# Second layer of a hybrid DiT step: three heads and a convolution projected ahead of the norm, and a norm in two VectorE instructions a tile

## The chip, the cores and the metric

One Trainium2 chip, one core. The metric is the device time of one launch in microseconds (us), the median of the runs of a kernel. Tiles are written partitions x elements.

## The reference

One inference step of a diffusion backbone: two layers, model width 1024, 384 tokens (128 context, 256 latent) that use the same weights but are modulated by two different vectors (two groups). Each layer norms its input and reads it through one input projection with three kinds of heads, adds their output projection, and then an MLP of width 4096 with a squared ReLU. All is float32.

```
h = _rmsnorm(x, norm_mix[d]) * (1.0 + c_scale) + c_shift
q, k, v, gb, gc, xin, u, vs = _project(h, w_in[d])
# latent tokens: rotary on q, k; cached context keys and values in front
att  = _diff_attention(q, k, v, lam, subln[d], lam_init)   # 4 heads, softmax of two halves, a0 - lam * a1
conv = gb * _short_conv(gc * xin, conv_w[d], conv_b[d])    # 256 channels, width 3
cmlp = _chunk_mlp(u, vs, w_s[d], b_s[d])
x = x + gate * (concat([att, conv, cmlp]) @ w_out[d])
h = _rmsnorm(x, norm_mlp[d]) * (1.0 + c_scale2) + c_shift2
x = x + gate2 * (relu(h @ w_up[d]) ** 2 @ w_down[d])
```

The outputs are the two normed token groups and the new context keys and values.

## The kernel before

Activations lie transposed, as 8 tiles of 128 features x 384 tokens. Float32 products are made of three float32r matmuls: an operand is split into a high part (a rounding cast) and a low part (operand minus high part), and `mm3` adds high·high, low·high and high·low. The split activation is held in `hh` (high) and `hl` (low). Weights are streamed in chunks of 512 KB, one for each 128 output columns of a projection: a DMA on SP's queue into one of six `raw` buffers, a ScalarE cast to `whi` (L201) and a VectorE subtraction to `wlo` (L203), four buffers each.

Each engine runs its instructions in the order in which the program writes them, and that order is made by hand. The TensorE stream is written straight down; after each product of three matmuls `tick` advances a clock, and work of the other engines, written as generators, is started with a delay in ticks (`start(gen, delay)`) and goes on when its `yield n` ticks have passed. The delays stand in the table `WAIT`, one number a layer. A projection of a 128-column tile (`proj_tiles`) has 8 ticks, one for each k tile of 128 features. The V projection (`proj_tokens(a, 512)`, tile `nat`) has tokens as rows: for each of 8 k tiles 9 matmuls of 512 columns, counted as 4 ticks, 72 matmuls and 32 ticks in all. It is evicted by three ScalarE copies into `v_t` (L887).

The norm. While the layer ahead ends, `scaled_high` and `scaled_low` put x·scale, split but not yet divided by the root mean square, into `hh` and `hl`, with two more columns for the shifts of the two groups (386 = `TE` columns). A projection of these, times rstd (a row over tokens), plus the projected shift, equals the projection of the normed input. So the key and query tiles `pkq` of the first `NPRE` heads are projected from the un-normed `hh`, `hl`, and `evict` multiplies by rstd. `normed` later replaces `hh`, `hl` by the normed input, tile by tile: on VectorE t = x·scale·rstd (two instructions, one a token group, L362), on ScalarE hh = t + shift (two, L370), on VectorE hl = t + shift − hh (two, L373). Whatever is projected behind that reads the normed input. In the second layer before the change, two heads (four `pkq` tiles) go ahead; `first_heads` adds their projected shifts on ScalarE (L706 to L712) and starts `keys` and `queries`: the rotary part (a VectorE shuffle and three GpSimd instructions), and the splits `kh`, `kl`, `qs` in halves of 64 partitions. Then follow V, the two later heads (`pk`, `pq`), and two convolutions (`pgc`, `pxi`, `pgb` for each).

Attention (`attention`) of a head is three units: 128 context queries, and twice 128 latent queries over 384 keys. A unit has scores `sc` in two PSUM buffers (two halves of the differential softmax), a VectorE maximum `nm`, ScalarE exps `e` with sums `s`, a ScalarE scaling of the second half, a VectorE combination of `e`, three TensorE transposes `pt`, and a ScalarE copy of them (`atp`, `ats`). The third unit goes on with `po`, the product with `v_t`, its norm and transpose. `sc` and `pt` share three PSUM buffers: unit 1's second score tile takes the first buffer of unit 0, and unit 2's two score tiles those of unit 1. The units of head h start at `unit0` + h·`head` ticks, 8 ticks apart.

The MLP's `hidden` evicts a tile of the up projection: VectorE copies the two shift columns to `ub` and multiplies by rstd, ScalarE applies ReLU with the shift as bias (two instructions), squares and casts.

Of the kernel before, what the change touches and what calls it, by code (L numbers as in the profile page):

```python
# [15 lines left out]
P = 128  # L16
# [3 lines left out]
TP = 128  # L20
# [8 lines left out]
NPRE = (3, 2)  # L29
# [33 lines left out]
    "fh0": (14, 14),  # L63
# [8 lines left out]
    "normed": (3, 3),  # L72
    "wait_normed": (1, 12),
    "mix": (4, 4),
    "heads": (4, 1),
# [5 lines left out]
    "head": (24, 24),  # L81
    "late": (0, 5),
# [18 lines left out]
def dit_kernel(ctx, tc, xT, cT, wmod, wmodT, wall, ck, cv, ws, lam, bs_in, small, rope, ident_in, yT, kT_out, v_out):  # L101
# [112 lines left out]
    def temp(name):  # L214
        return work.tile([P, T], F32, name=name, tag="tA", bufs=4)
# [129 lines left out]
    def rstd_of_x():  # L345
        pm = misc_tile("pstat")
        mm(pm[:, 0:T], ones_d, stat["acc"], start=True, stop=True)
        y = stat["rstd"] = work.tile([P, T], F32, name="rstd", bufs=1)
        yield 2
        nc.scalar.activation(y, pm[:, 0:T], AF.Ln)  # L350
        nc.scalar.activation(y, y, AF.Exp, scale=-0.5)
        yield 2
        a = work.tile([P, T], F32, name="rtmp", tag="rtmp", bufs=1)
        rsqrt_refined(y, a, pm[:, 0:T])

    def normed(scale, shift, every):


        def times(dt):
            t = temp("t")  # L360
            for g, a, b in GROUPS:
                nc.vector.scalar_tensor_tensor(  # L362
                    t[:, a:b], x[:, dt, a:b], scale[:, dt, g : g + 1], stat["rstd"][:, a:b], ALU.mult, ALU.mult
                )
            return t

        t = times(0)
        for dt in range(KT):
            for g, a, b in GROUPS:
                nc.scalar.activation(hh[:, dt, a:b], t[:, a:b], AF.Identity, bias=shift[:, dt, g : g + 1])  # L370
            ahead = times(dt + 1) if dt + 1 < KT else None
            for g, a, b in GROUPS:
                nc.vector.scalar_tensor_tensor(  # L373
                    hl[:, dt, a:b], t[:, a:b], shift[:, dt, g : g + 1], hh[:, dt, a:b].bitcast(F32),
                    ALU.add, ALU.subtract,
                )
# [132 lines left out]
    for d in range(DEPTH):  # L509
# [26 lines left out]

        if d == 0:
# [68 lines left out]
            start(shifted(), 1)  # L608
            start(steps(spread, 4, 3), wt["spread"])
            start(rstd_of_x(), wt["rstd"])  # L610
            q_t, k_t, v_t, cv_t, wsT, vsn = mixer_tiles()
# [12 lines left out]
        else:  # L624
# [20 lines left out]
        def split_y(i, yf):  # L645
            nc.scalar.copy(y[:, 0, i], yf)
            yield wt["sy"]
            nc.vector.tensor_sub(y[:, 1, i], yf, y[:, 0, i].bitcast(F32))

        LO, HI = slice(0, 64), slice(64, 128)  # L650
        parts = {}

        def rope_apply(t):
            rt = work.tile([P, 2, TS], F32, name="rt", tag="rope", bufs=1)
            s, t1 = rt[:, 0], rt[:, 1]
            nc.vector.stream_shuffle(s, t, [(i + 16) % 32 for i in range(32)])
            nc.gpsimd.tensor_mul(t1, t, rp[:, 0])
            nc.gpsimd.tensor_mul(s, s, rp[:, 1])  # L658
            nc.gpsimd.tensor_add(t, t1, s)

        def keys(h):


            k = k_t[:, h % 3]
            nc.sync.dma_start(k[:, TP : 2 * TP], ck[d, h])
            nc.sync.dma_start(kT_out[d, h], k[:, 0:TP])
            yield wt["k0"]
            rope_apply(k[:, 2 * TP :])
            yield wt["k1"]
            kh = work.tile([P, 2, T], F32R, name="kh")  # L670
            kl = kl_t[h % 2]
            parts[h] = [kh, kl]
            for c, own in enumerate((LO, HI)):
                nc.scalar.copy(kh[own, c], k[own, TP:])
            yield wt["k2"]
            for c, (own, other) in enumerate(((LO, HI), (HI, LO))):
                nc.scalar.copy(kh[other, c], k[own, TP:])
                nc.vector.tensor_sub(kl[own, c], k[own, TP:], kh[own, c].bitcast(F32))

        def queries(h):  # L680


            q = q_t[:, h % 3]
            yield wt["q0"]
            rope_apply(q[:, TP:T])
            yield wt["q1"]
            qs = work.tile([P, 2, TS], F32R, name="qs")
            parts[h].append(qs)
            for c, own in enumerate((LO, HI)):
                nc.scalar.copy(qs[own, c], q[own, TP:T])  # L690
            yield wt["q2"]
            for c, (own, other) in enumerate(((LO, HI), (HI, LO))):
                nc.vector.tensor_sub(qs[other, c], q[own, TP:T], qs[own, c].bitcast(F32))

        def first_heads():
            for h in range(NPRE[d]):
                if h != 1:
                    if d == 0:
                        yield from shift_products(raws, bias, 2 * h, 2 * h + 4 - h)
                    qb = bias[:, 2 * h + 1 : 2 * h + 4 - h : 2]  # L700
                    nc.vector.tensor_scalar_mul(qb, qb, 0.125)
                if h == 2:
                    yield wt["fh0"]
                for g, s0, s1, off in KSEG:
                    kk = k_t[:, h, off : off + s1 - s0]
                    nc.scalar.activation(kk, kk, AF.Identity, bias=bias[:, 2 * h, g : g + 1])  # L706
                go(keys(h))
                yield wt["fh1"]
                qb = bias[:, 2 * h + 1]
                for c, own in enumerate((LO, HI)):  # L710
                    nc.scalar.activation(qp_t[h % 3][own, c], q_t[own, h, 0:TP], AF.Identity, bias=qb[own, 0:1])
                nc.scalar.activation(q_t[:, h, TP:T], q_t[:, h, TP:T], AF.Identity, bias=qb[:, 1:2])  # L712
                yield wt["fh2"]
                go(queries(h))
                yield wt["fh3"]
# [118 lines left out]
        def conv(ct):  # L834

            pg = proj_tiles(a, name="pgc")
            gc = work.tile([P, T], F32, name="gc", tag="tB", bufs=2)
            nc.scalar.copy(gc, pg[:, 0:T])
            px = proj_tiles(a, name="pxi")
            cz = work.tile([P, T + 1], F32, name="cz", tag="tB", bufs=2)  # L840
            go(conv_input(ct, gc, px, cz))
            pb = proj_tiles(a, name="pgb")
            go(conv_output(ct, pb, cz))
# [26 lines left out]
        start(first_heads(), wt["heads"])  # L870
        if d == 0:
            nc.sync.dma_start(bs, bs_in)
# [39 lines left out]
        for f in range(2):  # L912
# [199 lines left out]
```

## Time and profile before

| | us |
|---|---|
| median of 3 runs | 909.0 (907.77 to 909.69) |
| profiled execution | 906.61 |
| its span, first to last instruction | 904.8 |
| mean granted TensorE clock | 0.995 |

| engine | busy us | share of the span |
|---|---|---|
| TensorE, matmuls | 876.9 | 97% |
| TensorE, weight loads (beside them) | 841.8 | 93% |
| VectorE | 651.6 | 72% |
| ScalarE | 481.7 | 53% |
| GpSimd | 84.2 | 9% |

In the profile's lines PE is TensorE, DVE VectorE, ACT ScalarE, POOL GpSimd, and SP the queue that issues DMAs. A row of groups has source line, engine, operation, tile written <- tiles read, shapes and count, then busy us and mean ns of one, then idle time of the engine just before them and what ended it. A row of waits has the engine, the tile at which it stood, what it waited for, then us in total, times and the longest. A row of the timeline has start us, length us, engine, line, operation and count. A row of windows has the stretch, its length, busy us (and instructions) of the engines, the granted clock as a share of full speed, the DMA share and GB/s. Matmul records overlap, so what one costs is the distance of starts. Source lines in rows of before are those of the kernel above.

The second layer's mixer runs from about 460 us on; its V projection and the norm beneath it lie around 480 to 510 us, the later heads and convolutions to about 570. The MLPs, about 200 to 450 and from 600 on, are the bulk of the time.

### The profile page before, as it was taken

How to read it: one execution, taken by the hardware profiler on the slowest of the kernel's cores; microseconds unless marked ns; L12 is line 12 of the kernel's file. 1: busy time of each engine (PE TensorE's matmuls, PEld its weight loads, DVE VectorE, ACT ScalarE, POOL GpSimd, SP SyncE). 2: the span in 40 equal slices, each digit the busy share in tenths (PEclk: the TensorE clock that was granted, in tenths of full speed). 3: DMA queues.
4: the chain of work that ended last, by engine and by line, in shares of the span. 5: the costliest groups of instructions: out<-in, count | busy, mean ns of one | idle time of the engine just before them, and what ended most of it. 6: DMA issues, size and time to landing. Idle time of an engine off the chain costs nothing.

```text
span 904.8 us, 14504 instructions
## 1 busy us (share of the span) xinstructions
PE 876.9 (97%) x5476; PEld 841.8 (93%) x5476; DVE 651.6 (72%) x1214; ACT 481.7 (53%) x949; POOL 84.2 (9%) x84
## 2 busy tenths in 40 slices
PE   5999989999999999999998999999999999999996
PEld 4867878999999999999997889999999999999996
DVE  5697887889888777889979877568886334555333
ACT  4568765447662236654336786444675223665331
POOL 1013310030000000000113340002000000000021
PEclk9999999999999999999999999999999999999998
DMA  9977657555667655557663323234565333433302
GB/s 346 330 280 258 231 168 271 167 166 167 205 190 235 230 187 190 197 189 236 213 218 102 131 73 117 92 97 134 175 220 167 123 133 117 133 124 118 116 1 70
DMA packets 48470, 156.55 MB, mean 173 GB/s; under 512 B 5392, under 2 KB 11024, under 8 KB 48400
## 3 DMA queue, kind: packets, MB, share of 16 engines
q1 hardware_dynamic: 48400, 155.63, 51.8%
q8 instruction: 43, 0.70, 0.3%
q14 instruction: 27, 0.22, 0.1%
HBM read 152.98 MB, written 2.62 MB: 172 GB/s over the span
## 4 chain that ended last, share of the span: by engine, by line
PE 84%; DVE 7%; ACT 4%; POOL 2%; issue 1%; DMA 1%; SPq 0%; DVEq 0%; ACTq 0%; POOLq 0%
PE pdn L220 10%; PE pdn L222 10%; PE pdn L221 10%; PE pup L221 10%; PE pup L220 9%; PE pup L222 9%; PE po L220 2%; PE po L221 2%; PE po L222 2%; PE pm L262 2%; PE pkq L220 2%; PE pkq L221 2%; PE pkq L222 1%; DVE wlo L203 1%; POOL rt L658 1%
## 5 line engine op out<-in xcount | busy, mean ns | idle before, releaser
L201 ACT CAST whi<-raw 128x1024 fp32r<-128x1024 f32 x182 | 190.4, 1052 | 286.8 <-PE pdn L221 153.9
L203 DVE TENSOR_TENSOR wlo<-raw,whi 128x1024 fp32r<-128x1024 f32 x182 | 224.6, 1240 | 61.4 <-ACT whi L201 61.2
L220 PE MATMUL pdn<-ah,whi 128*128 128x384 f32 (+2 forms) x528 | 174.7, 331 | 0.0
L221 PE MATMUL pdn<-al,whi 128*128 128x384 f32 (+2 forms) x528 | 174.6, 331 | 0.0
L222 PE MATMUL pdn<-ah,wlo 128*128 128x384 f32 (+2 forms) x528 | 174.6, 331 | 0.0
L220 PE MATMUL pup<-hh,whi 128*128 128x386 f32 x512 | 174.2, 340 | 0.0
L221 PE MATMUL pup<-hl,whi 128*128 128x386 f32 x512 | 173.7, 339 | 0.3
L222 PE MATMUL pup<-hh,wlo 128*128 128x386 f32 x512 | 172.8, 338 | 0.0
L315 DVE SCALAR_TENSOR_TENSOR junk<-raw,cb 128x1024 bf16<-128x1024 f32 x112 | 136.7, 1220 | 0.4
L221 PEld LDWEIGHTS pdn<-al,whi 128*128 128x128 f32 x528 | 99.2, 188 | 0.0
L220 PEld LDWEIGHTS pdn<-ah,whi 128*128 128x128 f32 x528 | 99.2, 188 | 0.0
L222 PEld LDWEIGHTS pdn<-ah,wlo 128*128 128x128 f32 x528 | 99.2, 188 | 0.0
L221 PEld LDWEIGHTS pup<-hl,whi 128*128 128x128 f32 x512 | 96.9, 189 | 1.1 <-DVE hl L388 0.9
L220 PEld LDWEIGHTS pup<-hh,whi 128*128 128x128 f32 x512 | 96.4, 188 | 0.3
L222 PEld LDWEIGHTS pup<-hh,wlo 128*128 128x128 f32 x512 | 96.5, 188 | 0.0
L337 POOL TENSOR_TENSOR sacc<-sacc,sq 128x384 f32<-128x384 f32 x23 | 29.6, 1285 | 667.5 <-ACT sq L330 533.6
L927 ACT ACTIVATE relu<-relu,ub 128x128 f32<-128x128 f32 (+1 forms) x128 | 51.3, 449 | 17.4 <-DVE relu L924 17.4
L399 DVE SCALAR_TENSOR_TENSOR x<-pdn,modv,x 128x128 f32<-128x128 f32 (+1 forms) x62 | 23.0, 413 | 43.9 <-PE pdn L222 43.9
L931 DVE TENSOR_TENSOR al<-relu,ah 128x384 fp32r<-128x384 f32 x64 | 35.6, 556 | 15.2 <-ACT ah L929 14.9
L220 PE MATMUL po<-y,whi 128*128 128x384 f32 x128 | 43.0, 336 | 0.0
L222 PE MATMUL po<-y,wlo 128*128 128x384 f32 x128 | 42.8, 334 | 0.0
L221 PE MATMUL po<-y,whi 128*128 128x384 f32 x128 | 42.8, 334 | 0.0
(202 smaller groups left out, 1413.7 us busy)
## 6 DMA issues: line engine op xcount, KB each, us to landing
raw<-in_wall_dram SPq DMA_DIRECT2D x182, 512.0 KB, 3.6
raw<-in_wmodT_dram SPq DMA_DIRECT2D x56, 512.0 KB, 4.3
raw<-in_wmod_dram SPq DMA_DIRECT2D x40, 512.0 KB, 5.7
raws<-in_wall_dram SPq DMA_DIRECT2D x6, 512.0 KB, 7.1
x<-in_xT_dram SPq DMA_DIRECT2D x8, 192.0 KB, 8.0
out_dram<-x SPq DMA_DIRECT2D x4, 256.0 KB, 2.6
mix<-in_cv_dram SPq DMA_DIRECT2D x2, 256.0 KB, 5.0
mix<-in_ws_dram SPq DMA_DIRECT2D x2, 256.0 KB, 5.2
```

What stands on the lines that cost most here:

```text
L201: nc.scalar.copy(hi, r)
L203: nc.vector.tensor_sub(lo, r, hi.bitcast(F32))
L220: mm(out, wh[wsl], ah[asl], start=first, stop=False)
L221: mm(out, wh[wsl], al[asl], start=False, stop=False)
L222: mm(out, wl[wsl], ah[asl], start=False, stop=last)
L262: mm(pm[32 * j : 32 * j + 32, own], sct[:, kt, :], w[:, (4 * k + j) * width : (4 * k + j + 1) * width], start=(kt == 0), stop=(kt == KT - 1),)
L315: nc.vector.scalar_tensor_tensor(junk, w, 1.0, cb[:, g], ALU.mult, ALU.mult, accum_out=mr[:, dt, g : g + 1])
L337: eng.tensor_add(stat["acc"], stat["acc"], sq)
L399: nc.vector.scalar_tensor_tensor(x[:, dt, a:b], pacc[:, a:b], gate[:, dt, g : g + 1], x[:, dt, a:b], ALU.mult, ALU.add)
L658: nc.gpsimd.tensor_mul(s, s, rp[:, 1])
L927: nc.scalar.activation(r[:, s0:s1], r[:, s0:s1], AF.Relu, bias=ub[:, g : g + 1])
L931: nc.vector.tensor_sub(al[:, i], r, ah[:, i].bitcast(F32))
```

## The change

In the second layer, `NPRE` goes from 2 to 3 heads, and convolution 0 is projected ahead of the norm too: its three tiles have 386 columns, and `with_norm` multiplies by rstd (VectorE) and adds the projected shift (two ScalarE instructions with a column of the tile itself as bias). So six `pkq` tiles and three convolution tiles stand ahead of the V projection, in which four `pkq` tiles stood ahead before, and the projections behind it are fewer by as many. The preparation of head 0 and head 1 starts right behind their pairs, that of head 2 32 ticks behind its pair. The norm starts 50 ticks (before: 12) behind the first two tiles, with 2 ticks a tile in place of 3, and units of attention start with V.

In both layers `normed` becomes: VectorE t = x·rstd, one instruction over 384 columns; ScalarE t = t·scale + shift in place, two instructions, each with two column operands; ScalarE hh = cast of t; VectorE hl = t − hh. So 2 VectorE instructions in place of 4, and 3 ScalarE instructions in place of 2. In `hidden` the copy to `ub` goes, since rstd gets two more columns of ones (a GpSimd memset) and the tile is multiplied over 386 columns. The weights lie in the changed order of use. Helpers that stood further down are moved up unchanged, and the body of `first_heads` becomes `first_head`.

```diff
-NPRE = (3, 2)
+NPRE = (3, 3)
...
-    "fh0": (14, 14),
+    "fh0": (14, 32),
...
-    "normed": (3, 3),
-    "wait_normed": (1, 12),
+    "normed": (3, 2),
+    "wait_normed": (1, 50),
...
-    "heads": (4, 1),
+    "heads": (4, 4),
...
-    "head": (24, 24),
-    "late": (0, 5),
+    "head": (24, 23),
+    "late": (0, 0),
...
+        stat["rstd1"] = work.tile([P, TE], F32, name="rstd", bufs=1)
+        nc.gpsimd.memset(stat["rstd1"][:, T:TE], 1.0)
+        y = stat["rstd"] = stat["rstd1"][:, 0:T]
...
         def times(dt):
             t = temp("t")
-            for g, a, b in GROUPS:
-                nc.vector.scalar_tensor_tensor(
-                    t[:, a:b], x[:, dt, a:b], scale[:, dt, g : g + 1], stat["rstd"][:, a:b], ALU.mult, ALU.mult
-                )
+            nc.vector.tensor_mul(t, x[:, dt], stat["rstd"])
             return t
 
         t = times(0)
         for dt in range(KT):
             for g, a, b in GROUPS:
-                nc.scalar.activation(hh[:, dt, a:b], t[:, a:b], AF.Identity, bias=shift[:, dt, g : g + 1])
+                nc.scalar.activation(
+                    t[:, a:b], t[:, a:b], AF.Identity, bias=shift[:, dt, g : g + 1], scale=scale[:, dt, g : g + 1]
+                )
+            nc.scalar.copy(hh[:, dt, 0:T], t)
             ahead = times(dt + 1) if dt + 1 < KT else None
-            for g, a, b in GROUPS:
-                nc.vector.scalar_tensor_tensor(
-                    hl[:, dt, a:b], t[:, a:b], shift[:, dt, g : g + 1], hh[:, dt, a:b].bitcast(F32),
-                    ALU.add, ALU.subtract,
-                )
+            nc.vector.tensor_sub(hl[:, dt, 0:T], t, hh[:, dt, 0:T].bitcast(F32))
...
             def evict_all(i):
                 nc.vector.tensor_copy(bias[:, i], pre[i][:, T:TE])
+                if i % 2 == 1:
+                    nc.vector.tensor_scalar_mul(bias[:, i], bias[:, i], 0.125)
                 evict(i)
 
             for i in range(2):
                 start(once(evict_all, i), 1 + i)
+            start(first_head(0), wt["heads"])
 
             def norm_part():
                 yield wt["wait_normed"]
                 yield from normed(amix[d], modv[d][:, 0], wt["normed"])
 
             start(norm_part())
-            for i in (2, 3):
+            for i in range(2, 2 * NPRE[d]):
                 pre.append(proj_tiles(a, 1, TE, "pkq", later=wt["later"]))
                 evict_all(i)
...
+                if i == 3:
+                    start(first_head(1), 1)
+            start(first_head(2), wt["fh0"])
...
+        def with_norm(t, pt):
+            nc.vector.tensor_mul(t, pt[:, 0:TE], stat["rstd1"])
+            for g, s0, s1 in GROUPS:
+                nc.scalar.activation(t[:, s0:s1], t[:, s0:s1], AF.Identity, bias=t[:, T + g : T + g + 1])
+        def after(gen, t, pt):
+            with_norm(t, pt)
+            yield 1
+            yield from gen
+        def conv(ct, pre=False):
+            cols = TE if pre else T
+            pg = proj_tiles(a, 1, cols, "pgc")
+            gc = work.tile([P, TE], F32, name="gc", tag="tB", bufs=2)
+            if pre:
+                with_norm(gc, pg)
+            else:
+                nc.scalar.copy(gc[:, 0:T], pg[:, 0:T])
+            px = proj_tiles(a, 1, cols, "pxi")
+            cz = work.tile([P, TE], F32, name="cz", tag="tB", bufs=2)[:, 0 : T + 1]
+            if pre:
+                xi = temp("xi", TE)
+                go(after(conv_input(ct, gc, xi, cz), xi, px))
+            else:
+                go(conv_input(ct, gc, px, cz))
+            pb = proj_tiles(a, 1, cols, "pgb")
+            if pre:
+                bf = temp("gb", TE)
+                go(after(conv_output(ct, bf, cz), bf, pb))
+            else:
+                go(conv_output(ct, pb, cz))
...
+        if d == 1:
+            y = wpool.tile([P, 2, KT, T], F32R, tag="hidH", name="y")
+            conv(0, True)
         nat = proj_tokens(a, 512)
         for i, pt in enumerate(nat):
             nc.scalar.copy(v_t[:, i, :], pt)
         nc.sync.dma_start(v_out[d], v_t[:, 0, :])
-        y = wpool.tile([P, 2, KT, T], F32R, tag="hidH", name="y")
         if d == 0:
+            y = wpool.tile([P, 2, KT, T], F32R, tag="hidH", name="y")
             conv(0)
         later_heads()
-        for ct in range(1 - d, 2):
-            conv(ct)
+        conv(1)
...
-                r = temp("relu")
-                ub = work.tile([P, 2], F32, name="ub")
-                nc.vector.tensor_copy(ub, pt[:, T:TE])
-                nc.vector.tensor_mul(r, pt[:, 0:T], stat["rstd"])
+                r = temp("relu", TE)
+                nc.vector.tensor_mul(r, pt[:, 0:TE], stat["rstd1"])
                 yield wt["hid0"]
                 for g, s0, s1 in GROUPS:
-                    nc.scalar.activation(r[:, s0:s1], r[:, s0:s1], AF.Relu, bias=ub[:, g : g + 1])
+                    nc.scalar.activation(r[:, s0:s1], r[:, s0:s1], AF.Relu, bias=r[:, T + g : T + g + 1])
+                r = r[:, 0:T]
...
-        chunks += kq[:n] + list(wv.reshape(4, P, 1024))
-        if d == 0:
-            chunks += convs[0] + kq[n:] + convs[1]
-        else:
-            chunks += kq[n:] + convs[0] + convs[1]
+        wv = list(wv.reshape(4, P, 1024))
+        chunks += kq[:n] + (wv + convs[0] if d == 0 else convs[0] + wv) + kq[n:] + convs[1]
```

The order on VectorE. Before, rows of the norm (t, then its low part hl; `modv`, `amix` are shift and scale) stand ahead of the eviction of head 1's queries and head 0's rotary part (`mix` is the store of keys, queries and values):

```order
L203 TENSOR_TENSOR wlo<-raw,whi 128x1024
L362 SCALAR_TENSOR_TENSOR t<-x,amix_94,rstd 128x128
L362 SCALAR_TENSOR_TENSOR t<-x,amix_94,rstd 128x256
L373 SCALAR_TENSOR_TENSOR hl<-t,modv_92,hh 128x128
L373 SCALAR_TENSOR_TENSOR hl<-t,modv_92,hh 128x256
L630 COPY bias_4927<-pkq 128x2
L522 SCALAR_TENSOR_TENSOR mix<-pkq,rstd 128x384
L701 TENSOR_SCALAR bias_4927<-bias_4927 128x2x2
L656 STREAM_SHUFFLE rt<-mix 128x256
```

Now they stand between the parts of convolution 0 (cz, gb); these are the rows around the start of V, with the number of each tile:

```order
L203 TENSOR_TENSOR wlo_5205<-raw_5202,whi_5204 128x1024
L364 TENSOR_TENSOR t_5225<-x_74,rstd_4898 128x384
L364 TENSOR_TENSOR t_5230<-x_74,rstd_4898 128x384
L375 TENSOR_TENSOR hl_98<-t_5225,hh_97 128x384
L364 TENSOR_TENSOR t_5243<-x_74,rstd_4898 128x384
L375 TENSOR_TENSOR hl_98<-t_5230,hh_97 128x384
L833 SCALAR_TENSOR_TENSOR cz_5207<-z_102,sm_75,cz_5207 128x385 x2
L364 TENSOR_TENSOR t_5257<-x_74,rstd_4898 128x384
L375 TENSOR_TENSOR hl_98<-t_5243,hh_97 128x384
L844 TENSOR_TENSOR gb_5272<-pgb_5212,rstd_4898 128x386
L364 TENSOR_TENSOR t_5285<-x_74,rstd_4898 128x384
L375 TENSOR_TENSOR hl_98<-t_5257,hh_97 128x384
```

A tile of the norm has half the rows, and the convolution and the attention stand among them where evictions and rotary parts stood.

The order on ScalarE, from the last tile of the norm to the first exps of unit 1 (e, s: exps and sums; nm: maximum) and the three V copies. Before:

```order
L370 ACTIVATE hh<-t,modv_92 128x128
L370 ACTIVATE hh<-t,modv_92 128x256
L674 CAST kh<-mix 64x384 x2
L677 CAST kh<-mix 64x384 x2
L201 CAST whi<-raw 128x1024
L751 ACTIVATE e,s<-sc,nm 128x128 x2
L690 CAST qs<-mix 64x256 x2
L757 ACTIVATE e<-e,s 128x128
L201 CAST whi<-raw 128x1024
L887 COPY mix<-nat 128x512 x3
L751 ACTIVATE e,s<-sc,nm 128x384 x2
```

Now, from the last tile of the norm on:

```order
L370 ACTIVATE t<-t,modv_92,amix_94 128x128
L370 ACTIVATE t<-t,modv_92,amix_94 128x256
L373 CAST hh<-t 128x384
L759 ACTIVATE e,s<-sc,nm 128x384 x2
L595 ACTIVATE qp_108<-mix,bias_4857 64x128 x2
L596 ACTIVATE mix<-mix,bias_4857 128x256
L765 ACTIVATE e<-e,s 128x384
L565 CAST kh<-mix 64x384 x2
L780 COPY atp<-pt 128x128
L201 CAST whi<-raw 128x1024
L568 CAST kh<-mix 64x384 x2
```

Here the exps of unit 1 stand right behind the norm's last tile, the preparation of head 2 (qp, mix, kh) follows, and unit 2, half of the next head's first units and two weight casts come ahead of the V copies; before, one unit of 128 keys stood ahead of them.

More of the change, by code (lines that the diff above doesn't have):

```diff
@@ L212, in misc_tile, with temp @@
         return ps.tile([P, 512], F32, tag="misc", name=name, bufs=3)
-    def temp(name):
-        return work.tile([P, T], F32, name=name, tag="tA", bufs=4)
+    def temp(name, cols=T):
+        return work.tile([P, TE], F32, name=name, tag="tA", bufs=4)[:, 0:cols]
     def mm3(out, w, a, wsl, asl, first, last):
@@ L535, in mixer_tiles, with split_y, rope_apply @@
             )
+        def split_y(i, yf):
+            nc.scalar.copy(y[:, 0, i], yf)
+            yield wt["sy"]
+            nc.vector.tensor_sub(y[:, 1, i], yf, y[:, 0, i].bitcast(F32))
+        LO, HI = slice(0, 64), slice(64, 128)
+        parts = {}
+        def rope_apply(t):
+            rt = work.tile([P, 2, TS], F32, name="rt", tag="rope", bufs=1)
+            s, t1 = rt[:, 0], rt[:, 1]
+            nc.vector.stream_shuffle(s, t, [(i + 16) % 32 for i in range(32)])
+            nc.gpsimd.tensor_mul(t1, t, rp[:, 0])
+            nc.gpsimd.tensor_mul(s, s, rp[:, 1])
+            nc.gpsimd.tensor_add(t, t1, s)
@@ new lines, in keys @@
+        def keys(h):
+            k = k_t[:, h % 3]
+            nc.sync.dma_start(k[:, TP : 2 * TP], ck[d, h])
+            nc.sync.dma_start(kT_out[d, h], k[:, 0:TP])
+            yield wt["k0"]
+            rope_apply(k[:, 2 * TP :])
+            yield wt["k1"]
+            kh = work.tile([P, 2, T], F32R, name="kh")
+            kl = kl_t[h % 2]
+            parts[h] = [kh, kl]
+            for c, own in enumerate((LO, HI)):
+                nc.scalar.copy(kh[own, c], k[own, TP:])
+            yield wt["k2"]
+            for c, (own, other) in enumerate(((LO, HI), (HI, LO))):
+                nc.scalar.copy(kh[other, c], k[own, TP:])
+                nc.vector.tensor_sub(kl[own, c], k[own, TP:], kh[own, c].bitcast(F32))
@@ new lines, in queries @@
+        def queries(h):
+            q = q_t[:, h % 3]
+            yield wt["q0"]
+            rope_apply(q[:, TP:T])
+            yield wt["q1"]
+            qs = work.tile([P, 2, TS], F32R, name="qs")
+            parts[h].append(qs)
+            for c, own in enumerate((LO, HI)):
+                nc.scalar.copy(qs[own, c], q[own, TP:T])
+            yield wt["q2"]
+            for c, (own, other) in enumerate(((LO, HI), (HI, LO))):
+                nc.vector.tensor_sub(qs[other, c], q[own, TP:T], qs[own, c].bitcast(F32))
@@ new lines, in first_head @@
+        def first_head(h):
+            for g, s0, s1, off in KSEG:
+                kk = k_t[:, h, off : off + s1 - s0]
+                nc.scalar.activation(kk, kk, AF.Identity, bias=bias[:, 2 * h, g : g + 1])
+            go(keys(h))
+            yield wt["fh1"]
+            qb = bias[:, 2 * h + 1]
+            for c, own in enumerate((LO, HI)):
+                nc.scalar.activation(qp_t[h % 3][own, c], q_t[own, h, 0:TP], AF.Identity, bias=qb[own, 0:1])
+            nc.scalar.activation(q_t[:, h, TP:T], q_t[:, h, TP:T], AF.Identity, bias=qb[:, 1:2])
+            yield wt["fh2"]
+            go(queries(h))
+            yield wt["fh3"]
@@ L539, in dit_kernel, with first_heads @@
+        def first_heads():
+            for h in range(NPRE[d]):
+                if h != 1:
+                    yield from shift_products(raws, bias, 2 * h, 2 * h + 4 - h)
+                    qb = bias[:, 2 * h + 1 : 2 * h + 4 - h : 2]
+                    nc.vector.tensor_scalar_mul(qb, qb, 0.125)
+                if h == 2:
+                    yield wt["fh0"]
+                yield from first_head(h)
         if d == 0:
@@ L661, in keys @@
[L661 to L693, printed above, removed]
@@ L695, in first_heads @@
-        def first_heads():
-            for h in range(NPRE[d]):
-                if h != 1:
-                    if d == 0:
[L699 to L715, printed above, removed]
+                if i == 3:
+                    start(first_head(1), 1)
@@ L869, in dit_kernel @@
         nc.sync.dma_start(wsT, ws[d])
-        start(first_heads(), wt["heads"])
         if d == 0:
+            start(first_heads(), wt["heads"])
             nc.sync.dma_start(bs, bs_in)
@@ L962, in dit_kernel @@
     gate = modv[DEPTH - 1][:, 5]
-    y = work.tile([P, T], F32, name="rstd", bufs=1)
+    y = work.tile([P, TE], F32, name="rstd", bufs=1)[:, 0:T]
     newton = work.tile([P, T], F32, name="rtmp", tag="rtmp", bufs=1)
```

26 lines of the change are left out of this document (1 added, 25 removed).

## The prediction

> **What bounds the kernel now.** First I read the engines' totals on the page, then windows of the second layer's mixer, then what TensorE waits for there, then single records.
>
> ```profile
> PE 876.9 (97%) x5476; PEld 841.8 (93%) x5476; DVE 651.6 (72%) x1214; ACT 481.7 (53%) x949; POOL 84.2 (9%) x84
> ```
>
> TensorE's stream is the kernel: a change pays where TensorE stands still, costs where it makes it stand, and does nothing elsewhere. The windows (TensorE, weight loads, VectorE, ScalarE, GpSimd busy; clock; DMA) cover the second layer's mixer, a stretch of MLP, and the first layer's norm.
>
> ```profile
> 480.00:500.00 20.00, 17.21 (x79) 14.11 (x78) 19.95 (x45) 15.47 (x34) 8.12 (x9) 0.98 0.36 114
> 500.00:520.00 20.00, 19.57 (x102) 17.40 (x101) 17.19 (x37) 15.15 (x37) 6.25 (x7) 0.93 0.35 122
> 520.00:540.00 20.00, 17.98 (x109) 16.99 (x108) 15.52 (x36) 17.39 (x49) 9.46 (x9) 1.00 0.26 83
> ...
> 640.00:660.00 20.00, 20.00 (x115) 1.00 0.55 180
> ...
> 48.00:66.00 18.00, 18.00 (x116) 12.65 (x115) 17.12 (x47) 11.94 (x27) 2.43 (x3) 1.00 0.70 261
> ```
>
> From 480 to 540 TensorE is idle 60 − 54.76 = 5.2 us. VectorE is the full engine (19.95 of 20) while the norm runs under the V projection; ScalarE has 4.5 us free. The longest wait of that stretch and the records behind it:
>
> ```profile
> PE nat L451 <- DVE hl L373: 2.8, 1, 2.8
> ```
> ```profile
> 500.39 0.77 PE L449 MATMUL nat<-whi,hh 128*128 128x512 f32 x1
> ...
> 502.95 0.39 PE L449 MATMUL nat<-whi,hh 128*128 128x512 f32 x1
> ...
> 503.88 0.39 PE L450 MATMUL nat<-wlo,hh 128*128 128x512 f32 x1
> ```
> ```profile
> 498.00:501.00 3.00, 3.00 (x13) 2.54 (x13) 2.97 (x8) 2.98 (x8) 2.19 (x3) 0.73 0.41 161
> ```
>
> It, 2.8 us, is for the low part of a normed tile. Behind it the granted clock is 0.73, and six 512-column matmuls take 502.95 − 500.39 = 2.56 us where four take 0.93 at full clock (0.2325 each, so 1.4): 1.2 lost, with 0.1 in the scores ahead some 1.3. **At stake: 5.2 + 1.3 = 6.5 us**, of which 2.0 lie in 520–540, behind the V projection.
>
> **The change part by part.** Work that leaves no TensorE idle is free: the MLP's 64 VectorE copies go (10.2 us by the row below), but TensorE is busy 20.00 of 20 there, so I count 0. TensorE's matmul count is the same; 120 matmuls grow from 384 to 386 columns, at 20/115 = 0.174 us each 0.1 us in all. Weight chunks change order, not number. On SP, the last early head's key store now stands ahead of three weight loads and waits for its ScalarE rows; with six raw buffers and a DMA share of 0.36 I cost it at 0, at most one load.
>
> The layer-1 norm gains a cast a tile on ScalarE. It was free 18 − 11.94 = 6.1 us of that window, TensorE never waited in it, and VectorE gets work off: 0, bounds −0.5 and +1.
>
> The rest hangs on ScalarE from the first normed tile of layer 2 to the three V copies, which stand ahead of the first attention product `po`. Its prices, by shape:
>
> ```profile
> L201 ACT CAST whi<-raw 128x1024 fp32r<-128x1024 f32 x12 | 12.6, 1047 | 2.9 <-PE pkq L221 2.8
> L751 ACT ACTIVATE e<-sc,nm 128x384 f32<-128x384 f32 x8 | 4.6, 596 | 0.0
> L677 ACT CAST kh<-mix 64x384 fp32r<-64x384 f32 x8 | 4.1, 513 | 0.1
> L674 ACT CAST kh<-mix 64x384 fp32r<-64x384 f32 x8 | 4.1, 511 | 1.0 <-PE sc L741 0.6 <-POOL mix L659 0.4
> L370 ACT ACTIVATE hh<-t,modv 128x256 fp32r<-128x256 f32 x8 | 4.0, 505 | 0.0
> L690 ACT CAST qs<-mix 64x256 fp32r<-64x256 f32 x8 | 3.2, 404 | 2.5 <-POOL mix L659 2.4
> L370 ACT ACTIVATE hh<-t,modv 128x128 fp32r<-128x128 f32 x8 | 3.2, 399 | 2.5 <-DVE t L362 2.3 <-PE pkq L222 0.2
> L751 ACT ACTIVATION_READ_ACCUMULATOR e<-sc,nm 128x1 f32 x14 | 2.9, 207 | 0.0
> L757 ACT ACTIVATE e<-e,s 128x384 f32<-128x384 f32 x4 | 2.5, 619 | 2.3 <-DVE s L756 2.3
> L751 ACT ACTIVATE e<-sc,nm 128x128 f32<-128x128 f32 x6 | 2.2, 363 | 2.9 <-DVE nm L746 2.9
> L774 ACT COPY ats<-pt 128x384 f32<-128x384 f32 x4 | 1.9, 481 | 0.1
> L711 ACT ACTIVATE qp<-mix,bias 64x128 f32<-64x128 f32 x4 | 1.6, 400 | 0.0
> L887 ACT COPY mix<-nat 128x512 f32<-128x512 f32 x3 | 1.6, 591 | 0.0
> L757 ACT ACTIVATE e<-e,s 128x128 f32<-128x128 f32 x3 | 1.2, 405 | 0.8 <-DVE s L756 0.8
> ...
> L822 ACT ACTIVATE cz<-z,sm 128x385 f32<-128x385 f32 x1 | 0.7, 712 | 0.0
> L810 ACT ACTIVATE y<-pot,subg 128x384 fp32r<-128x384 f32 x1 | 0.6, 586 | 0.0
> ```
>
> The new norm tile does what the MLP does on ScalarE: a pair in place, then an instruction that needs both, then a cast.
>
> ```profile
> 212.38 0.52 ACT L929 CAST ah<-relu 128x384 fp32r<-128x384 f32 x1
> 212.80 0.80 ACT L927 ACTIVATE relu<-relu,ub 128x128 f32<-128x128 f32 x2
> 213.64 0.53 ACT L928 ACTIVATE relu<-relu 128x384 f32<-128x384 f32 x1
> ```
>
> The pair with the wait behind it takes 213.64 − 212.80 = 0.84, a cast 212.80 − 212.38 = 0.42, so independent neighbours overlap by 0.10. A tile is 1.26, eight are 10.1. By the changed order the stretch also holds, at the mean less 0.10: five weight casts 4.7, exps with their reads 4 × 0.60 and 4 × 0.37 = 3.9, scalings 2 × 0.52 and 2 × 0.31 = 1.7, `cz` 0.6, two `ats` 0.8, V copies 1.5; at the full mean the half-partition rows `kh`, `qs`, `qp` 3.7; gate, bias and small copies, taken as their nearest shapes above, 2.4. **Sum 29.4 us.** TensorE's own work from the start of V to `po`: 72 × 0.2325 = 16.7, twelve score matmuls of 384 columns 2.1, and small ones and three of the next head, an estimate from those pitches, 2.1: **20.9 us**. ScalarE can begin some 0.6 us before V: the xi product ends eight ticks (eight times three matmuls at 0.174, 4.2 us) ahead of it, and its eviction, gate product and a weight split stand on VectorE before the first x·rstd. So **at least 29.4 − 0.6 − 20.9 = 7.9 us** of standing are new, if ScalarE never waits.
>
> It does wait, since VectorE alternates with it:
>
> ```profile
> L203 DVE TENSOR_TENSOR wlo<-raw,whi 128x1024 fp32r<-128x1024 f32 x182 | 224.6, 1240 | 61.4 <-ACT whi L201 61.2
> ...
> L931 DVE TENSOR_TENSOR al<-relu,ah 128x384 fp32r<-128x384 f32 x64 | 35.6, 556 | 15.2 <-ACT ah L929 14.9
> ...
> L923 DVE COPY ub<-pup 128x2 f32<-128x2 f32 x64 | 10.2, 159 | 39.3 <-PE pup L222 39.0 <-ACT relu L927 0.3
> ```
>
> I laid the rows of both engines one behind the other in the changed order, V's start being 0. ScalarE reaches the first exp after four norm tiles 5.0, `cz`, a weight cast and the gate 2.3, two waits of about 0.9 on VectorE (gate product behind two `cz` rows; maximum behind the fourth low part) and the exp, 0.4, from −0.6 on: 8.9. TensorE wants that score buffer back at 5.3 for the second tile of unit 1 (start 0.3, two k tiles 4.2, scores, low-part waits): **3.6**. It is at unit 0's transpose at 11.5, whose weights leave VectorE at 14.6, behind a weight split and two low parts: **3.1**. Unit 2's scores want both buffers of unit 1 at 17.0; its exps stand behind the eighth norm tile and end at 20.5, with the first of the scores run by then: **3.2**. Then 0.5 at unit 1's transpose, 1.3 at the next head's scores, 2.0 at `po` for the V copies, which stand behind a scaling, a transpose copy and a weight cast. With 0.3 at the start: **14.0 us**, 6.1 above the bound; I take it, since the pairs must alternate in this order, and keep 7.9 as the other end. Of the 2.0 behind V (520–540) I keep half, between 0 and 2: one head's preparation fewer is left there, the attention chain is the same.
>
> Each normed ACTIVATE now has scale and bias as operands. Rows: 586 ns with one (384 columns), 712 with two (385); 16 × 0.1 = 1.6 us, taken as 0 because ScalarE idles some 5 us in the 14.0, with 1.6 as upper end. The Trainium skill, page "ScalarE: Activation LUTs", section "What ACT_TABLE_LOAD costs", gives about 93 ns per [128,1] pointer operand, an estimate of 1.5 us for the 16; the two rows agree, and by the page the sum would be +10.0 in place of +8.5.
>
> **Sum:** −6.5 + 14.0 + 1.0 = **+8.5 us**. Against the profiled execution (906.6, of it 904.8 span) that is 915.1; the timed median, 909.0, lies 2.4 above, so I predict **917.5**. Its own range: half of the 6.1 is not lost, +5.4; pointers 1.6, another 1.3 of slow clock and the other 1.0 behind V, +12.4: 914.4 to 921.4.
>
> **Rivals.**
> 1. *ScalarE bounds, but waits nowhere.* VectorE's row falls from four instructions a tile to two and keeps ahead. −6.5 + 7.9 + 1.0 = +2.4, with pointers +4.0: 911.4 to 913.0. For: VectorE was the full engine. Against: its rows between the norm's (splits of 1.24, convolution, maxima) are still in line.
> 2. *Faster: the hidden norm.* In the V projection ScalarE passes its rows in TensorE's 20.9 us, so only the 2.8 us wait and the slow clock go, with all but 1.0 of the rest: −5.5, 903.5. It decides from the point where the stretch's rows sum to 21.5 rather than 29.4, say if weight casts and head 2's preparation were done earlier. Against: ScalarE keeps its order, and the V copies are last.
> 3. *A cold clock.* Gaps of 3.6, 3.1 and 3.2 us are each as long as the one that gave 0.73; 1.3 each is hidden by the next wait, except after the last two: +2.6 on the forecast, 920.1. The Trainium skill, page "TensorE: Matmul & The Clock Gate", Part 1, says one idle window of about 3.4 us drops the clock to half; the trace shows 0.73 over 3 us after 2.8.
> 4. *The change does nothing that lasts:* the gain of 6.5 and a new bound of some 6.5 cancel, 908 to 910.5, if my prices are a tenth high.
>
> **How the numbers follow.** Forecast 0.57, rival 1 0.15, rival 2 0.13, rival 3 0.08, rival 4 0.07. A measurement tells about 0.2% (1.8 us) from nothing: below 907.2 rival 2, 0.13; within, rival 4 with a little of rival 1, 0.08; above, 0.79. The range 906 to 922 leaves out most of rival 2 and a tail above.
>
> **What would show it.** In the changed profile: ScalarE near 100% over the V projection with VectorE below it; TensorE waiting at `sc` for `e`, at `pt` for the weighted `e`, at `po` for the V copies, each 2 to 4 us; no wait of 2.8 at `nat` for `hl`; the MLP at 100% TensorE and layer 1 as before. It would be wrong if ScalarE shows idle time over V while TensorE runs, if `po` waits for nothing, or if the stretch from V's start to `po` lasts under 28 us.

## The result, and the profile after

The change makes the kernel slower: 924.7 us (median of 4 runs, 922.84 to 925.72) against 909.12 (907.77 to 909.69), a ratio of 1.0171 with a 95% interval of 1.015 to 1.0192. That is +15.6 us where +8.5 was forecast. The profiled execution of the change took 925.72.

The engine totals of the changed kernel, from the page:

```profile
PE 883.8 (96%) x5476; PEld 847.3 (92%) x5476; DVE 642.3 (70%) x1128; ACT 493.3 (53%) x970; POOL 83.3 (9%) x88
```

TensorE runs as many matmuls as before and the span is 18.8 us longer. VectorE lost 9.3 us, ScalarE gained 11.6. Where the time went is best read from starts of the same matmuls in both traces (us; a stretch is between two starts):

| stretch | before | change | longer by |
|---|---|---|---|
| start to first V product of layer 1 | 50.50 | 52.66 | 2.2 |
| from there to the layer's first up product | 146.07 | 152.31 | 6.2 |
| from there to layer 2's first key product | 269.61 | 269.59 | 0 |
| from there to layer 2's first up product | 155.99 | 166.14 | 10.2 |

So the MLP is untouched, the second layer's mixer loses 10.2 us, and the first layer's mixer, forecast at 0, is 6.2 us longer. Part of these 6.2 us is clock that the profile of before happened to keep; the last section takes it apart. Windows of the changed kernel over the second layer's V projection (which starts at 514 and meets `po` at 549) and over 83 to 89 us in the first layer; columns as before:

```profile
500.00:520.00 20.00, 18.85 (x101) 17.31 (x99) 14.14 (x25) 11.45 (x21) 0.79 (x1) 1.00 0.33 114
520.00:540.00 20.00, 11.81 (x44) 8.80 (x45) 13.27 (x32) 16.91 (x40) 5.88 (x6) 0.91 0.16 57
540.00:560.00 20.00, 18.66 (x106) 16.31 (x105) 13.11 (x31) 14.42 (x43) 2.93 (x3) 1.00 0.29 97
...
83.00:86.00 3.00, 2.18 (x8) 2.18 (x9) 2.87 (x9) 2.89 (x6) 0.00 (x0) 0.50 0.54 209
86.00:89.00 3.00, 3.00 (x11) 3.00 (x10) 2.06 (x6) 1.92 (x6) 0.00 (x0) 0.50 0.62 232
```

From 520 to 540 TensorE stands 8.2 us while ScalarE is the fullest engine; VectorE is no longer full. In the first layer the clock is half for 6 us. The longest waits of TensorE in 470 to 650:

```profile
PE sc L749 <- ACT e L759: 6.7, 2, 3.9
PE pt L771 <- DVE e L767: 2.4, 1, 2.4
PE pt L771 <- ACT hh L373: 1.8, 1, 1.8
PE po L794 <- ACT mix L921: 1.1, 1, 1.1
PE po L794 <- ACT ats L782: 0.7, 1, 0.7
PE nat L448 <- ACT hh L373: 0.6, 1, 0.6
```

The wait of 2.8 us at `nat` for `hl` is gone, as forecast, and scores, transposes and `po` wait in its place. The same waits as single records (in brackets the idle time):

```profile
514.58 0.50 PE L448 MATMUL nat<-whi,hh 128*128 128x512 f32 x1 [0.64 <-ACT hh L373]
...
523.34 0.69 PE L749 MATMUL sc<-kh,qs 128*128 128x384 f32 x1 [3.86 <-ACT e L759]
...
529.30 0.30 PE L771 MATMUL pt<-ident,e 128*128 128x128 f32 x1 [1.79 <-ACT hh L373]
...
534.48 0.45 PE L749 MATMUL sc<-kh,qs 128*128 128x384 f32 x1 [2.81 <-ACT e L759]
...
548.89 0.49 PE L794 MATMUL po<-mix,atp 128*128 128x128 f32 x2 [1.09 <-ACT mix L921]
```

V's first product would have started at 514.58 − 0.64 = 513.94; `po` starts at 548.89, 34.95 us later. With TensorE's own 20.9 that is 14.05 us of standing and slow clock, where 14.0 was forecast. How far that is the forecast's own sum, and how far luck, is told below. ScalarE, over the same stretch, idles for VectorE where the forecast had it (0.8 us each at the gate product and at the maximum, forecast as about 0.9), and once more at the next unit's maximum:

```profile
519.78 0.80 ACT L846 ACTIVATE gb<-gb 128x128 f32<-128x128 f32 x2 [0.83 <-DVE gb L844]
...
522.83 0.37 ACT L759 ACTIVATE e<-sc,nm 128x128 f32<-128x128 f32 x1 [0.83 <-DVE nm L754]
...
533.76 0.58 ACT L759 ACTIVATE e<-sc,nm 128x384 f32<-128x384 f32 x1 [1.43 <-DVE nm L754]
```

From its first normed tile (513.00) to the V copies (548.25) it idles 5.3 us in all and is busy 29.9, where the forecast had some 5 and 29.4.

### The profile page after: what moved, and what is told of

It is laid out like the page before. It is cut to its first block, busy times and chain, and to the rows that moved or that the text cites. A ratio compares the mean times of both kernels' runs of the same rounds, so it can differ in the third digit from the quotient of the medians.

```text
span 923.6 us, 14506 instructions
## 1 busy us (share of the span) xinstructions
PE 883.8 (96%) x5476; PEld 847.3 (92%) x5476; DVE 642.3 (70%) x1128; ACT 493.3 (53%) x970; POOL 83.3 (9%) x88
## 4 chain that ended last, share of the span: by engine, by line
PE 81%; DVE 7%; ACT 7%; issue 2%; POOL 2%; DMA 1%; SPq 0%; DVEq 0%; ACTq 0%; POOLq 0%
PE pdn L221 10%; PE pdn L222 10%; PE pdn L220 10%; PE pup L221 9%; PE pup L220 9%; PE pup L222 9%; PE po L222 2%; PE po L221 2%; PE po L220 2%; DVE wlo L203 2%; PE pkq L220 2%; PE pkq L221 2%; ACT whi L201 2%; PE pkq L222 2%; PE pm L262 1%
## 5 line engine op out<-in xcount | busy, mean ns | idle before, releaser
L955 DVE TENSOR_TENSOR relu<-pup,rstd 128x386 f32<-128x386 f32 x64 | 35.5, 558 | 41.3 <-PE pup L222 41.1
L958 ACT ACTIVATE relu<-relu 128x128 f32<-128x128 f32 (+1 forms) x128 | 51.1, 447 | 15.0 <-DVE relu L955 15.0
L220 PE MATMUL po<-y,whi 128*128 128x384 f32 x128 | 43.0, 336 | 0.0
```

Of the source, the lines that this page charges most:

```text
L220: mm(out, wh[wsl], ah[asl], start=first, stop=False)
L955: nc.vector.tensor_mul(r, pt[:, 0:TE], stat["rstd1"])
L958: nc.scalar.activation(r[:, s0:s1], r[:, s0:s1], AF.Relu, bias=r[:, T + g : T + g + 1])
```

## The experiments

All medians and intervals against runs of the kernel before on the same chip. "Layer 1" is the stretch from its first V product to its first up product, "layer 2" the one from its first key product to its first up product, both in the profiled execution.

| run | median us | ratio, 95% interval | layer 1 | layer 2 |
|---|---|---|---|---|
| before (profile) | 908.8 to 909.6 | | 146.1 | 156.0 |
| the change | 924.7 | 1.0150 to 1.0192 | 152.3 | 166.1 |
| l1_old_norm | 921.1 | 1.0099 to 1.0162 | 148.7 | 166.2 |
| l1_new_norm | 912.85 | 1.0029 to 1.0059 | 151.2 | 155.9 |
| old_norm_both | 917.56 | 1.0057 to 1.0109 | 147.0 | 164.3 |
| units_later | 923.09 | 1.0125 to 1.0183 | 151.2 | 166.4 |
| norm_4_ticks | 923.2 | 1.0140 to 1.0179 | 149.7 | 165.7 |
| mlp_part | 909.64 | 0.9990 to 1.0010 | 148.6 | 156.0 |
| early_head | 925.0 | 1.0157 to 1.0188 | 148.6 | 171.0 |
| early_head_old_norm | 918.87 | 1.0065 to 1.0130 | 146.0 | 163.6 |
| l2_new_norm | 910.78 | 1.0000 to 1.0027 | 147.4 | 157.2 |
| conv_behind | 923.41 | 1.0131 to 1.0174 | 148.7 | 169.3 |
| own_tiles | 908.91 | 0.9983 to 1.0012 | 148.6 | 155.6 |
| units_behind | 909.86 | 0.9997 to 1.0023 | 148.7 | 155.2 |
| units_early | 909.68 | 1.0001 to 1.0030 | 145.9 | 158.0 |
| norm_lead | 905.99 | 0.9951 to 0.9975 | 145.9 | 152.4 |

**The first layer's norm.** Two mirrored runs, the four-instruction norm put back there, and the new one alone put into the kernel before:

```diff
-                yield from normed(amix[d], modv[d][:, 0], wt["normed"])      # layer 1, of the change
+                yield from normed_old(amix[d], modv[d][:, 0], wt["normed"])  # the function of before
```

> The changed kernel with the four-instruction norm of before in the first layer alone. Theory A: the first layer's norm loads ScalarE by about 0.7 us a tile (two ACTIVATEs of two operands and a cast, 1.43 us from start to start in the trace of the change, against 0.75), 5.5 us in all, which makes the copy for the bias products late and halves TensorE's clock behind it; then 918 to 920, and no PE wait of over 1.2 us at psb. Rival B: the first layer's 8 us in the profile are a late start of this one execution (its first product was 1.2 us later) and loading; then 924 to 925.

> The kernel before with the new norm in the first layer alone, the mirror of the run above. Theory A: 914 to 916, with psb waiting for the copy by 2 us or more and a granted clock of 0.5 to 0.7 behind it. Rival B: 908.5 to 909.5.

The change falls from 924.7 to 921.1 without it, and the kernel before rises by 4.0 (908.82 to 912.85, interval 2.6 to 5.4) with it: theory A, though smaller than its figures (921.1 lies between the two theories, 912.85 under A's range), and rival B falls. One sign of A did not come: with the old norm back, TensorE still waits 1.62 us at `psb`, where A had at most 1.2. In the traces the two norms lie apart: over the twelve profiles with the old norm in this layer the stretch takes 145.9 to 148.7 us, over the four with the new one 149.7 to 152.3. ScalarE's records of one tile in the change, and of two pairs of before:

```profile
50.55 0.99 ACT L370 ACTIVATE t<-t,modv,amix 128x128 f32<-128x128 f32 x2 [3.25 <-DVE t L364]
51.56 0.51 ACT L373 CAST hh<-t 128x384 fp32r<-128x384 f32 x1
51.98 1.05 ACT L201 CAST whi<-raw 128x1024 fp32r<-128x1024 f32 x1
```
```profile
62.59 0.79 ACT L370 ACTIVATE hh<-t,modv 128x128 fp32r<-128x128 f32 x2
63.29 0.82 ACT L711 ACTIVATE qp<-mix,bias 64x128 f32<-64x128 f32 x2
```

A tile is 51.98 − 50.55 = 1.43 us where the pair of before is 0.70. The copy `shb`, for which the bias products `psb` wait, stands behind the norm on ScalarE and is late. TensorE's wait for it in 40 to 160 us of l1_new_norm, and the clock behind it:

```profile
PE psb L493 <- ACT shb L489: 2.6, 2, 1.7
```
```profile
83.00:86.00 3.00, 3.00 (x12) 3.00 (x13) 2.81 (x7) 2.98 (x8) 0.00 (x0) 0.60 0.33 121
```

Before had one such wait of 1.1 us, with no slow clock behind it:

```profile
79.12 0.61 PE L472 MATMUL psb<-sel,shb 128*128 128x2 f32 x4 [1.13 <-ACT shb L468]
```

**The norm's form in the second layer.** In the change's order, and in the order of before:

> The changed order with the four-instruction norm of before in both layers. The first layer as in l1_old_norm. In the second, theory A (ScalarE bounds the V projection, as predicted): ScalarE has 8 x 0.7 = 5.5 us less there, VectorE about 3 us more; half of the second layer's loss goes, 913 to 916. Rival C: the loss is the alternation with VectorE, which has more to do now; 918 or more, the sc and pt waits as long as in the change.

> The kernel before, in its order, with the new norm in the second layer alone. VectorE loses about 0.4 us a tile, ScalarE gains 0.7. Theory A (both engines alternate over V, and what one gains the other loses): within 2 us of before, 907 to 911, the 2.8 us wait for hl smaller and waits for hh in its place. The rival, that VectorE's full stretch alone held V: 905 or less.

In the layer's trace the old form is worth 166.2 − 164.3 = 1.9 us in the change's order, and the new one costs 1.2 in the old order. (The medians of l1_old_norm and old_norm_both are 3.5 us apart; 1.6 of it is the first layer, 148.7 against 147.0, whose code is the same in both. old_norm_both's 917.56 lies between its two theories.) Both engines are in the loop: what VectorE gains, ScalarE loses. In l2_new_norm V waits 2.2 us for `hl` in place of 2.8, and 1.1 for `hh`. So 8 of the 10 us come from the order.

**The MLP's part alone** (no `ub`, rstd with two columns of ones):

> The kernel before with the MLP's part of the change alone (no copy to ub, rstd with two columns of ones, a GpSimd memset). As predicted: 0, 908 to 910; the rival, that VectorE's 10.2 us of copies held TensorE somewhere, gives 905 or less.

No difference, as costed.

**Which part of the order?** Attention 12 ticks later; the norm at half its pace; convolution 0 not ahead:

```diff
-    "fh0": (14, 32), "unit0": (24, 24), "head": (24, 23),
+    "fh0": (14, 44), "unit0": (24, 36), "head": (24, 20),   # units_later
-    "normed": (3, 2),
+    "normed": (3, 4),                                       # norm_4_ticks
```
```diff
-            conv(0, True)          # ahead of V
         later_heads()
+        if d == 1:
+            conv(0)                # conv_behind; unit0 1, fh0 8, wait_normed 26
         conv(1)
```

> The changed kernel with the second layer's attention 12 ticks later (first unit three k tiles into V, heads 20 ticks apart, so that the last one starts 3 ticks later, head 2's preparation 12 ticks later). Theory A (the norm and the first units want ScalarE in the same stretch): the waits at the scores of 3.9 and 2.8 us shrink, 917 to 921. Rival D: ScalarE's sum to the V copies decides wherever the units stand, and the waits only move: 923 to 926.

> The changed kernel with 4 ticks a tile in the second layer's norm in place of 2, which is V's own pace, so that the exps of units 0 and 1 stand between the norm's tiles on ScalarE and not behind them. Theory E (what costs is that the norm's rows are written into the queues ahead of attention's, though they take 16 us for their 14 ticks): the score waits of 3.9 and 2.8 us go, V waits for hh a little at each tile; 915 to 920. Theory A (ScalarE's sum to the V copies bounds): the waits change their place and the time stays, 922 to 926.

> As l1_old_norm (921.1), with convolution 0 of the second layer behind the later head instead of ahead of the norm; the norm, head 2's preparation and the units keep their places against V. V then carries no convolution tail (ScalarE 2 us, VectorE 4 us less), and three more tiles stand behind it. Theory A: 917 to 919, the score waits shorter by that tail. The rival, that attention's start with V is what costs: 920 to 922.

None helps: theories A of units_later and conv_behind fall (conv_behind lies above its rival's range too), and theory E of norm_4_ticks. The waits only change their place. At the norm's half pace the long score waits are gone and the transposes wait:

```profile
PE pt L771 <- DVE e L767: 7.7, 4, 2.9
PE nat L448 <- ACT hh L373: 2.8, 4, 0.9
```

Without the convolution ahead the layer even takes 3 us more (169.3 against 166.2 in l1_old_norm), so its tail in V is not the cause either.

**Head 0's units ahead of the norm**, beside convolution 0, with the new and with the old norm in layer 2 (the old one in layer 1):

```diff
-            yield wt["at6"]
+            yield wt["at6"] + ((26, 2, 0, 0)[h] if d == 1 else 0)   # po waits for V
-            start(units(h), wt["unit0"] + wt["head"] * h + (wt["late"] if h > 1 else 0))
+            start(units(h), (0, (1, 36, 58, 80))[d][h] if d == 1 else wt["unit0"] + wt["head"] * h)
```

> The changed order with the first layer's norm as before, and with head 0's three units beside convolution 0, ahead of the norm (its po waits until V is there), head 2's preparation 22 ticks earlier and head 1 in the second half of V. Theory A: ScalarE's rows from the first norm tile to the V copies fall from about 31 us to 26, so V takes 27 us in place of 32.5 in the second layer, 914 to 917 against 921.1 for the same without it. If the order of rows alone decides, less than 1 us is gained: 920 to 922.

> As early_head, with the four-instruction norm in both layers: ScalarE's rows to the V copies come to about 20.5 us, TensorE's own work there. Theory A: 909 to 913. If VectorE, which has 3 us more, now bounds: 915 or more.

Theory A misses in both, early_head by 8 us; early_head_old_norm came out where its other reading, that VectorE bounds, had it (915 or more). On VectorE the last unit's maximum and head 2's shuffle now stand ahead of the first x·rstd, which ends the idle time of 3.4 us that ScalarE has in early_head ahead of its first normed tile, and V starts late:

```profile
PE nat L473 <- ACT hh L398: 4.5, 1, 4.5
PE sc L774 <- ACT e L784: 4.2, 1, 4.2
```

Counting ScalarE's rows was not enough: attention ahead of the norm delays it too, through both engines.

**More room for the norm in the kernel before**: the first two k tiles of the normed input get buffers of their own and are normed 11 ticks earlier.

> The kernel before with buffers of their own for the first two k tiles of the second layer's normed input (6 KB a partition), which are normed beside the last two key and query tiles, 11 ticks earlier. If the 2.8 us wait for hl and the slow clock behind it come from the norm starting only when the un-normed tiles are read: 905 to 906.5. If VectorE, full from 480 to 506, only moves its queue: 908.5 to 909.5.

The time stays. The wait for `hl` is gone from `nat`, and the scores wait 4.0 us for `e` instead:

```profile
PE sc L755 <- ACT e L765: 4.0, 1, 4.0
PE po L800 <- ACT ats L788: 0.7, 1, 0.7
```

**Attention out of the norm's stretch.** Three heads ahead and the new norm stay; units come about as late against V as in the kernel before. Two more things move with them: head 2's preparation starts 24 ticks later, and convolution 0 must stand between V and head 3's pair, since head 3 takes head 0's key and query buffers (`h % 3`):

```diff
-            start(units(h), wt["unit0"] + wt["head"] * h + (wt["late"] if h > 1 else 0))
+            start(units(h), (24, 48, 72, 94)[h] if d == 1 else wt["unit0"] + wt["head"] * h)
+        if d == 1:
+            conv(0)
         later_heads()
-        if d == 1:
-            conv(0)
         conv(1)
```

> As conv_behind (923.4), with three heads ahead and the new norm in the second layer, but attention no earlier against V than in the kernel before: units start 24, 48, 72 and 94 ticks behind V's start in place of 1, 24, 47 and 70, head 2's preparation 24 ticks later, and convolution 0 stands right behind V, ahead of head 3's pair, whose buffers head 0 must have left. Theory G (what costs is attention's rows in the same stretch as the norm's): V with what follows to convolution 0 takes 24 to 26 us in place of 37, and the whole 909 to 914. Theory H (three heads ahead or the norm's form cost by themselves): 919 or more.

> The kernel before with the second layer's first attention head 8 ticks earlier (two units beside V and its norm in place of one), nothing else. Theory G: V gets longer by one unit's ScalarE and VectorE rows, some 2 to 3 us, of which part comes back behind V: 910 to 912. Theory H: 908.5 to 909.5.

units_behind takes 909.86, 13.5 less than conv_behind, and its second layer 155.2 in place of 169.3. From V's first product to the first one of the next projection it takes 517.00 − 497.80 = 19.2 us, where the expectation had 24 to 26, conv_behind takes 37.4, and V's 72 products alone are 16.7. Convolution 0 stands outside that stretch in both runs, so its place is not what frees the 18.2 us; some 4 come back behind V (from there to the up projection 107.7 in place of 103.7). Theory G holds so far: the third head and the new norm together cost nothing here; attention's rows beside the norm's do. Head 2's preparation left the stretch with the units, and its share is not told apart. The mirror, units_early, moves nothing but units: with one unit more beside the norm, that stretch goes from 23.4 us in before to 26.5, and the layer from 156.0 to 158.0; the median rises by 0.3 alone, less than G's size. TensorE's waits in 440 to 660 of units_behind, the first two:

```profile
PE nat L473 <- ACT hh L398: 2.0, 1, 2.0
PE pmix L906 <- ACT mix L956: 1.0, 1, 1.0
```

**A version that beats both.** units_behind with the first tile's product and ACTIVATEs 8 ticks earlier, only its cast waiting for the un-normed tile to be read, and the chunk products 2 ticks later:

```diff
         t = times(0)
+        modulate(0, t)
+        yield 8
         for dt in range(KT):
-            modulate(dt, t)
+            if dt:
+                modulate(dt, t)
             nc.scalar.copy(hh[:, dt, 0:T], t)
```

> units_behind with the first normed tile's product and its two ACTIVATEs 8 ticks earlier (only its cast waits until the un-normed tile is read), and the chunk products 2 ticks later. If the 2.0 us wait for hh at V's start and the 1.0 us at pmix are all that is left to gain there: 907 to 908, below before by 1.5 to 2.5. If the wait only moves to the second tile: 909 to 910.

905.99, a ratio of 0.9963 (0.9951 to 0.9975), below its expectation of 907 to 908. V's longest wait is now 0.7, and with the units away the new norm runs nearly in V's shadow, no engine full:

```profile
PE nat L481 <- DVE hl L406: 0.7, 1, 0.7
```
```profile
480.00:500.00 20.00, 19.16 (x100) 17.56 (x100) 17.70 (x39) 17.48 (x35) 9.53 (x12) 1.00 0.37 121
500.00:520.00 20.00, 19.56 (x93) 16.19 (x93) 13.97 (x27) 16.45 (x36) 3.05 (x4) 1.00 0.47 153
```

## Why the prediction was right and where it was wrong

The direction and the mechanism of the second layer were right, the sum was not, and the time came out above the range.

- **The step that failed: the layer-1 norm, costed "0, bounds −0.5 and +1".** It measured +4.0 alone (2.6 to 5.4) and −3.6 when taken out of the change. The reason given was that ScalarE was free 6.1 us of 48 to 66 and TensorE never waited there. But 0.73 us a tile (1.43 against 0.70) is 5.8 us, which leaves no room to spare, and the room did not even take it. The change's norm starts 2.3 us later; over the 18 us from the same point on, ScalarE is busy 13.8, 1.9 more than before, since it still waits for VectorE (0.8, 1.8 and 1.2 us). The norm then takes 21.1 us from its first row to its last (50.55 to 71.62) where before took 17.8 (48.24 to 66.00). The exps and `shb`, in line behind it, come late. TensorE then waits 2.6 us at `psb` and 1.0 at the scores, where before had 1.1 at `psb`: 2.5 us more. The trace of before held that wait of 1.1; I took it for unchanged. The clock behind such a wait, 0.50 for 6 us in the change, was left out as well, but it falls behind the old norm too (last section).

```profile
50.31:68.31 18.00, 17.14 (x111) 11.63 (x110) 12.05 (x27) 13.83 (x28) 0.72 (x1) 1.00 0.76 274
```
```profile
PE psb L471 <- ACT shb L467: 2.6, 2, 1.8
...
PE sc L749 <- ACT e L759: 1.0, 1, 1.0
```

- **The V term, 14.0, came out at 14.05, in part by luck.** Its waits are where it put them, but they sum to 10.6: at the scores 3.6 and 3.2 measured 3.9 and 2.8, at the transposes 3.1 and 0.5 measured 1.8 and 0.2, the next head's scores' 1.3 measured 0.2, the start's 0.3 measured 0.6, `po`'s 2.0 measured 1.1. The other 3.4 were not in the sum. Some 1.5 are slow clock, which I had only as a rival: from 523.34 to 526.64, behind the longest wait, two score matmuls and six of 512 columns take 3.30 us where at the usual distances of 0.174 and 0.2325 they take 1.74. The rest is what the small matmuls and the first ones behind a wait took above the estimate of 20.9.
- **Behind V, 1.0 was too small.** Idle time there was 0.9 in 560 to 580 and 2.2 in 580 to 600, mostly one transpose (2.4, for the combined `e`). Fewer tiles are left behind V to cover attention; that this is the reason was not tried by itself. So the layer is −6.5 + 14.05 + 3.1 = 10.65, measured 10.2.
- **The pointers, "taken as 0".** The pair with its dependent successor went from 0.84 to 51.56 − 50.55 = 1.01, so 0.17 for two, 1.4 us in 16, close to the estimate of 1.5 worked out from the Trainium skill's "ScalarE: Activation LUTs", section "What ACT_TABLE_LOAD costs". What it cost in time was not measured apart.
- **Rivals.** ScalarE without waits (911 to 913) fell: it idles for VectorE. The hidden norm (903.5) fell for this order; norm_lead, with attention moved away, comes part of the way (3.2 us below before, of the 5.5 it forecast). That gain and bound cancel fell. The cold clock held in part: it fell once within V, not behind each wait.
- **A reading that was incomplete:** I named ScalarE the bound, near 100% over V. It is busy 16.9 of the 20 us from 520 on. old_norm_both took some 5.8 us off it (8 tiles of 0.73) and gained 1.9; what bounds is the alternation of both engines over norm and attention. units_behind shows the stretch to be the cause, with head 2's preparation not told apart; units_early shows the same direction for attention alone. That the third head's buffers force attention there is read from the code, not measured.

Parts: above before, the medians of the change, l1_old_norm and old_norm_both are 15.6, 12.3 and 8.7 us. Taken off one after the other, the norm in layer 1 is 3.3, the norm's form in layer 2 3.5, and the order in layer 2 8.7. The form's 3.5 holds 1.6 of difference in the first layer, where nothing was changed between the two, so 1.9 is the better figure for it.

## What to carry to other kernels

Idle time of an engine in a window covers added work only if the rows can run in it, with room to spare; here they waited for other engines and came out later. Price the next rows in line too, and above all a wait that is there already. When two stages both alternate between ScalarE and VectorE, don't lay them in one stretch: another spacing did not help here, a cheaper form gained 1.9 us, and moving one of them away (with the third head's preparation) gained 13.5. Work that is pulled ahead may also take cover from what it is pulled past; that was not tried by itself.

## What the runs showed that was not expected

- The clock falls after short gaps, though not after every one, and equal gaps differ. Behind the wait at the first layer's `psb` it stayed 1.00 after 1.13 us (before) and 1.56 us (old_norm_both), and fell to 0.67 over 81 to 84 after 1.36 us (l2_new_norm). With 0.99 and 1.79 us and four matmuls between, it was 0.50 for 6 us in the change; with 0.99 and 1.78 us it stayed 1.00 in norm_4_ticks. The Trainium skill, page "TensorE: Matmul & The Clock Gate", Part 1, has a free-running window of about 3.4 us whose position varies; that would fit, but no run here shows the window.
- With the old norm in the first layer, the stretch from its V to the up projection takes anything from 145.9 to 148.7 us (table), though its code is all but the same, and runs of the kernel before spread from 906.2 to 911.4. The clock sorts the profiles. In 45 to 201 us, in windows of 3 us, it falls below 0.97 at two places at most, behind the wait at `psb` and behind a later one at `po`. Where it falls at neither, the old norm takes 145.9 to 146.1 (four profiles, before among them), at one 147.0 and 147.4, at both 148.6 to 148.7 (six). The new norm takes 149.7 where it falls at one (norm_4_ticks) and 151.2, 151.2 and 152.3 at both. So at an equal clock the new norm costs some 2.5 us (3.7 in the change's own profile), about as much as TensorE waits longer for ScalarE, and the rest of the 6.2 us in the first table is clock. A single profile can be nearly 3 us off by this alone.
